# Gate modulation rows on TensorE, one inverse chain for both superchunks, and bonus products on ScalarE and GpSimd

## The chip, the cores and the metric

The kernel runs on one core of a Trainium2 chip (trn2). A core has a matrix engine (TensorE, PE in the profile), a vector engine (VectorE, DVE), a scalar engine (ScalarE, ACT), a general one (GpSimd, POOL) and a queue that issues transfers (SyncE, SP); each has its own instruction stream, and they meet at semaphores. Matrices come from HBM to SBUF (128 partitions) by DMA, and matmuls write to PSUM, of which there are eight banks of 128 x 512 floats. The metric is device time in microseconds, the median of several runs; smaller is better.

## What is computed

One layer of a network on 256 tokens of 1024 channels, in float32: a modulation from a conditioning vector c (twelve rows of 512 values, `silu(c) @ w_ada + b_ada`), a mixing block of which one half of the channels goes through a recurrence (RWKV-7) and the other through attention, a mixture of 32 experts with top 4, and a last block with memory. What the change touches is the following.

```python
# modulation: six vectors of 1024 values (twelve rows of 512)
ada = silu(c) @ w_ada + b_ada       # shift1, scale1, gate1, shift2, scale2, gate2
x = x + gate1 * mix(rms_norm(x) * (1 + scale1) + shift1)
h = rms_norm(x) * (1 + scale2) + shift2
x = x + gate2 * experts(h)

# recurrence, per head, over 256 steps
state = (state * w_t + (state @ -kk_t) x (kk_t * a_t) + v_t x k_t)
y_t = state @ r_t
bonus = sum(r * k * r_k, axis=-1) * v
y = (norm(y) + bonus) * g
```

The recurrence is computed in chunks: within one, the steps depend on each other through a lower triangular matrix, which has to be inverted.

## The kernel before

**Stages.** `phase1` does everything up to the routing, in about 300 us; then the experts run, whose weights (192 tiles of 2 MB) stream through SBUF, and then the last block. A tile scheduler orders the instructions of each engine from the program; a pool with `bufs=n` gives a tile n buffers, and a tile's next use waits until its last reader is done. All weight tiles go through `stream` (L138), which issues one 2 MB transfer on SyncE's queue into a ring of three buffers.

**Modulation.** `ada_rows` (L278) makes up to four of the twelve rows at once on TensorE. For each row it streams a 1024 x 512 piece of w_ada and issues eight matmuls, 128 x 32 weights against 128 x 512 (L285), one group of 32 PSUM partitions for each k mod 4; scw holds silu(c) in one column among zeros, so that row i lands in partition i of its group. A first matmul (L280) puts the bias in, and ScalarE copies the bank to SBUF. This serves rows 0 to 3 at the start (`ra` and its second call) and rows 6 to 9 (`r1`) after the projections. Rows 4, 5, 10 and 11, the two gates, are made otherwise, in `gate_rows` (L295): VectorE makes 4 and 10 with a product and seven fused multiply-adds of 128 x 512 into gacc (L307, L305), and GpSimd makes 5 and 11 with eight products (L307) and seven sums (L309). gacc is 8 KB in each partition. What is left over the partitions is summed and spread by a matmul with ones (`gate_bc`, L316), at the end of the attention block.

**Projections.** `dense_T` and `dense_N` multiply the input (split into two parts hh and hl) by a 1024 x 512 piece of w_in. For each of eight k the piece is split: ScalarE rounds it (wsh, L145) and VectorE, or for each fourth one GpSimd, makes the residue (wsl, L146); then three products go to TensorE (L396 to L399, L411 to L413). The order is the LoRA columns, k, r, v, then the attention's q, k and v. The LoRA weights wua and gup (L441 to L443) feed small matmuls lo (L453) and g (L461), whose results go through sigmoids and exponentials on ScalarE.

**Recurrence.** It has two superchunks s of 128 tokens. `sub` (L537) makes the triangular products of each; its 16 x 16 diagonal blocks are inverted by `invert(s, r)` (L556), r from 0 to 14: TensorE spreads row r (row, L565, with a selector sel that GpSimd makes, L564), and VectorE does a product (L570) and a sum (L572), each 128 x 8(15 - r). The two chains alternate. `sub2(s)` (L645) transposes v, a, b and k (tr, L658; b and k after a VectorE product dc, L653), makes the masked products (lk, L534 to L669), and more products lv, yv and zk; `solve(s)` (L694) does the rest of the inverse with f (L710) and u (L720), and the state follows. Attention heads (sc, pt, po) run between. The bonus product prod is four VectorE instructions (L639).

**After it.** `w_out` multiplies by the output weights, the gates are applied, `choose` and `rank` do the routing. SyncE's queue has by then issued nine tiles of expert weights; the tenth stands behind a load of the largest count of the routing into a register (L978, `values_load`), which decides a branch later on.

Of the kernel before, what the change touches and what calls it, by code (L numbers as in the profile page):

```python
# [10 lines left out]
F32 = mybir.dt.float32  # L11
# [3 lines left out]
AF = mybir.ActivationFunctionType  # L15
OP = mybir.AluOpType
# [3 lines left out]
T, D = 256, 1024  # L20
# [2 lines left out]
BIG = 3.0e38  # L23

SIG_MAX = 1.0 / (1.0 + math.exp(-1.702 * 7.0))


NP, B4, NZ, ME = 4, 5, 5, 12
# [91 lines left out]
class Kernel:  # L120
# [133 lines left out]
    def phase1(self):  # L254
# [23 lines left out]
        def ada_rows(cis):  # L278
# [11 lines left out]
            r = p1.tile([128, 512], F32, tag="ar", name="ar")  # L290
# [4 lines left out]
        sc = scw[:, :, 32]  # L295

        def gate_rows():

            for q, i in enumerate((4, 5, 10, 11)):
                w = self.stream(A["w_ada"][:, i * 512:(i + 1) * 512].rearrange("(k p) f -> p k f", p=128), 8, 512)  # L300
# [9 lines left out]
                r = slice(32 * q, 32 * q + 1)  # L310
                eng.tensor_tensor(o[r], o[r], self.gate2[r, 512:1024], op=OP.add)

        def gate_bc(q):
# [13 lines left out]

        xn = pxn.tile([128, 2, D], F32, tag="xn", name="xn")
        ss = p1.tile([128, 2], F32, tag="ss", name="ss")
        for q, i in enumerate((4, 5, 10, 11)):  # L330
# [207 lines left out]
        def sub(s):  # L538

            tt = slice(s * 128, s * 128 + 128)  # L540
            L16 = pb.tile([128, 8, 128], F32, tag="L16", name="L16")
            Lof = pb.tile([128, 8, 128], F32, tag="Lof", name="Lof", bufs=2)
            for p, ps in pairs(aT, bT, tt, "lab"):
                DVE.tensor_tensor(par(L16, p), ps, bc("m16", 4), op=OP.mult)
                DVE.tensor_tensor(par(Lof, p), ps, bc("moff", 4), op=OP.mult)
            Lc = pb.tile([128, 8, 16], F32, tag=f"Lc{s}", name="Lc")
# [3 lines left out]
            ACT.activation(Lc.rearrange("p h q -> p (h q)"), ps[:, 0:128], AF.Copy)  # L550

            Tc = pb.tile([128, 8, 16], F32, tag=f"Tc{s}", name="Tc")
            POOL.tensor_copy(Tc, e16[:, None, :].to_broadcast([128, 8, 16]))
            return Lof, Lc, Tc

        def invert(s, r):  # L556

            Lof, Lc, Tc = parts[s]
            if r % 4 == 0:
                rows[s] = self.psum("row", chain=True)  # L560
                for q in range(r, min(r + 4, 15)):
                    if s == 0:
                        sel[q] = pb.tile([128, 128], F32, tag="sel", name="sel", bufs=5)
                        POOL.tensor_scalar(sel[q], blk16, e16[:, q:q + 1], None, op0=OP.mult)  # L564
                    PE.matmul(rows[s][:, (q % 4) * 128:(q % 4) * 128 + 128], sel[q], Lc.rearrange("p h q -> p (h q)"),  # L565
                              start=True, stop=True, skip_group_check=True)
            n = 15 - r
            t = pb.tile([128, 8, 16], F32, tag=f"tq{s}", name="tq")
            o = (r % 4) * 128
            DVE.tensor_tensor(t[:, :, 0:n], rows[s][:, o:o + 128].rearrange("p (h q) -> p h q", h=8)[:, :, r + 1:16],  # L570
                              Tc[:, :, r:r + 1].to_broadcast([128, 8, n]), op=OP.mult)
            DVE.tensor_tensor(Tc[:, :, r + 1:16], Tc[:, :, r + 1:16], t[:, :, 0:n], op=OP.add)  # L572

        parts = [sub(s) for s in range(2)]
        parts2, rows, sel = {}, {}, {}
        for r in range(15):
            for s in range(2):
                invert(s, r)


        qn, kn2 = Y[:, 0], Y[:, 1]
# [54 lines left out]
        POOL.tensor_tensor(wr, wr, sc2[:, :, None].to_broadcast([128, 8, NE]), op=OP.mult)  # L636

        for m in range(4):
            DVE.scalar_tensor_tensor(prod[:, m], rT[:, m], self.v("rk", m), kT[:, m], op0=OP.mult, op1=OP.mult)  # L639

        pb1 = right("pb1", eC)
        big4 = lambda n: pb1.tile([128, 8, 128], F32, tag="b4", name=n, bufs=B4)
# [49 lines left out]
            return nat["b"], R, Lrb  # L692

        def solve(s):  # L694
            Lof, Lc, Tc = parts[s]
            nb, R, Lrb = parts2[s]
            D2 = big4("Dt")
            Dt = D2.rearrange("p h (b q) -> p h b q", q=16)
            for hf in range(2):
                hsl = slice(4 * hf, 4 * hf + 4)  # L700
                (POOL if hf else DVE).tensor_tensor(
                    Dt[:, hsl], Tc[:, hsl, None, :].to_broadcast([128, 4, 8, 16]),
                    blk16.rearrange("p (b q) -> p b q", q=16)[:, None].to_broadcast([128, 4, 8, 16]), op=OP.mult)
            Ft, Rp = big4("Ft"), big4("Rp")
            R2 = R.rearrange("p h a j -> p h (a j)")
# [181 lines left out]
                todo = []  # L887

        w_out((4, 5, 6, 7))
        for dst, q in ((gate, 0), (self.gate2, 2)):  # L890
            for h in range(2):
                ACT.activation(dst[:, h * 512:(h + 1) * 512], gate_bc(q + h), AF.Copy)
        eN.close()
        e2s.close()
        w_out((0, 1, 2, 3))
# [722 lines left out]
```

## Time and profile before

| what | value |
|---|---|
| median of 3 runs | 1542.88 us (1541.7 to 1546.55) |
| the profiled execution | 1553.07 us, of which the span is 1551.3 us |
| TensorE busy | 1425.1 us, 92% of the span |
| VectorE busy | 570.8 us, 37% |
| ScalarE busy | 396.5 us, 26% |
| GpSimd busy | 213.0 us, 14% |
| transfers | 505.17 MB, mean 326 GB/s |

The profile is of one execution, and it is 10.2 us longer than the median. Its page cuts the span into 40 slices of 38.8 us. The first seven and a half hold `phase1`, the next 23 the experts, the rest the last block. In a timeline row the first two numbers are the start and the length in us, the count after x is that of the instructions put together, and a bracket at the end tells how long the engine was idle ahead and what released it. TensorE records a float32 matmul as two instructions here, so x16 is eight matmuls. The granted clock (PEclk) is a share of full speed: 1.00 is 2.4 GHz and 0.50 is 1.2 GHz.

### The profile page before, as it was taken

The numbers are of one execution on the slowest core, as the hardware profiler recorded it, in microseconds if no ns is written. First come the engines' busy times: TensorE is split into PE (matmuls) and PEld (weight loads), VectorE is DVE, ScalarE is ACT, GpSimd is POOL, SyncE is SP. The second block draws the span as 40 slices with busy tenths as digits, with TensorE's granted clock in tenths as the row PEclk, the third lists the DMA queues.
The fourth block names the chain that finished last, engine by engine and source line by source line (L and its number), as shares of the span: only waits on it lengthen the run. The fifth ranks groups of instructions, "written<-read, shape, count | busy, mean of one in ns | idle before, by whom it ended". The sixth has DMA issues, their size and how long they took to land. (4 is left out here: it accounts for less than half of the span.)

```text
span 1551.3 us, 19123 instructions
## 1 busy us (share of the span) xinstructions
PE 1425.1 (92%) x7818; PEld 824.2 (53%) x7818; DVE 570.8 (37%) x1144; ACT 396.5 (26%) x767; POOL 213.0 (14%) x190
## 2 busy tenths in 40 slices
PE   5999999899999999888888879999998899899996
PEld 2976887533443344233233234443332597699995
DVE  3576766522222222122122122121211345565445
ACT  4862244200100000000000011110100466455553
POOL 1244751000000000000000000000000343252221
PEclk8999789899999999999999999999999999999998
DMA  9835726799999999999999999999999741535440
GB/s 332 271 109 177 261 78 259 326 429 427 428 427 429 426 429 426 427 429 427 428 429 426 427 421 428 428 427 428 428 426 426 269 164 55 217 111 210 169 164 28
DMA packets 74599, 505.17 MB, mean 326 GB/s; under 512 B 5661, under 2 KB 6685, under 8 KB 50025
## 3 DMA queue, kind: packets, MB, share of 16 engines
q1 hardware_dynamic: 74328, 503.74, 79.6%
q8 instruction: 63, 1.03, 0.3%
q14 instruction: 32, 0.25, 0.0%
q0 software_dynamic: 176, 0.14, 0.0%
HBM read 502.82 MB, written 1.05 MB: 325 GB/s over the span
## 5 line engine op out<-in xcount | busy, mean ns | idle before, releaser
L114 PE MATMUL pg<-w,xe 128*64 128x512 f32 x1024 | 270.5, 598 | 42.6 <-DMA w<-w_gate_up 42.1
L114 PE MATMUL pu<-w,xe 128*64 128x512 f32 x1024 | 268.2, 594 | 0.0
L114 PE MATMUL py<-w,at 128*64 128x512 f32 x1024 | 228.8, 599 | 23.8 <-ACT at L1167 20.6
L1155 ACT ACTIVATE sg<-pg 128x512 f32<-128x512 f32 (+1 forms) x33 | 19.3, 586 | 664.9 <-PE pg L114 663.2
L1156 DVE TENSOR_SCALAR u<-pu 128x512 f32<-128x512 f32 (+1 forms) x33 | 22.2, 676 | 450.7 <-PE pu L114 450.7
L114 PEld LDWEIGHTS pg<-w,xe 128*64 128x64 f32 x1024 | 71.6, 137 | 189.4 <-issue 116.4
L114 PEld LDWEIGHTS py<-w,at 128*64 128x64 f32 x1024 | 71.1, 137 | 158.7 <-issue 130.2
L114 PEld LDWEIGHTS pu<-w,xe 128*64 128x64 f32 x1024 | 75.4, 137 | 146.1 <-issue 145.9
L145 ACT ACTIVATE w3h<-w 128x512 fp32r<-128x512 f32 x184 | 115.4, 631 | 108.6 <-PE d L1309 57.8
L146 DVE TENSOR_TENSOR w3l<-w,w3h 128x512 fp32r<-128x512 f32 x132 | 97.1, 741 | 111.2 <-ACT w3h L145 106.2
L146 POOL TENSOR_TENSOR w3l<-w,w3h 128x512 fp32r<-128x512 f32 x52 | 67.5, 1303 | 421.5 <-ACT w3h L145 410.2
L1180 DVE TENSOR_TENSOR y<-py,gate 64x512 f32<-64x512 f32 x64 | 44.0, 688 | 207.8 <-PE py L114 207.0
L1309 PE MATMUL d<-xl,w3h 128*128 128x256 f32 x352 | 99.6, 284 | 0.4 <-DVE xl L1297 0.4
L1308 PE MATMUL d<-xh,w3h 128*128 128x256 f32 x352 | 99.0, 283 | 1.0 <-ACT xh L1295 1.0
L1310 PE MATMUL d<-xh,w3l 128*128 128x256 f32 x352 | 99.3, 283 | 0.0
L1244 POOL TENSOR_TENSOR wml<-w,wml 128x512 fp32r<-128x512 f32 x4 | 5.1, 1279 | 679.1 <-ACT wml L1243 679.1
L114 PEld LDWEIGHTS ga<-s,xm 128*128 128x128 f32 x512 | 63.2, 201 | 13.5 <-issue 11.9
L1308 PEld LDWEIGHTS d<-xh,w3h 128*128 128x128 f32 x352 | 67.3, 192 | 1.6 <-ACT xh L1295 1.3
L1309 PEld LDWEIGHTS d<-xl,w3h 128*128 128x128 f32 x352 | 67.5, 192 | 1.0 <-DVE xl L1297 0.6
L1310 PEld LDWEIGHTS d<-xh,w3l 128*128 128x128 f32 x352 | 67.4, 192 | 0.2 <-DVE w3l L146 0.2
L114 PE MATMUL ga<-s,xm 128*128 128x128 f32 x512 | 66.3, 289 | 1.2 <-DVE s L1106 1.2
L114 PE MATMUL cb<-y,swt 128*128 128x512 f32 x128 | 59.2, 605 | 0.8 <-DVE y L1180 0.8
(420 smaller groups left out, 2078.5 us busy)
## 6 DMA issues: line engine op xcount, KB each, us to landing
w<-w_gate_up SPq DMA_DIRECT2D x128, 2048.0 KB, 30.5
w<-w_down SPq DMA_DIRECT2D x71, 2048.0 KB, 27.4
w<-w_ada SPq DMA_DIRECT2D x12, 2048.0 KB, 9.2
w<-w_up SPq DMA_DIRECT2D x8, 2048.0 KB, 7.5
w<-w_in SPq DMA_DIRECT2D x6, 2048.0 KB, 12.8
w<-w_in_sb SPq DMA_DIRECT2D x5, 2048.0 KB, 16.6
w<-w_out SPq DMA_DIRECT2D x4, 2048.0 KB, 7.7
w<-w_mem_kv SPq DMA_DIRECT2D x1, 2048.0 KB
```

The source lines that it names most:

```text
L114: return self._keep(self.tc.nc.tensor.matmul(*a, **k))
L145: self.nc.scalar.activation(hi, src, AF.Copy)
L146: eng.tensor_tensor(lo, src, hi.bitcast(F32), op=OP.subtract)
L1155: ACT.activation(cut(s, c), cut(pg, c), AF.Sigmoid, scale=1.702)
L1156: DVE.tensor_scalar(cut(u, c), cut(pu, c), 8.0, -6.0, op0=OP.min, op1=OP.max)
L1180: DVE.tensor_tensor(st[e & ~1][2][r, hs], py[64 * h:64 * h + 64], self.gate2[64 * h:64 * h + 64, hs], op=OP.mult)
L1244: (POOL if k % 2 else DVE).tensor_tensor(wl, w[:, k], wh.bitcast(F32), op=OP.subtract)
L1308: PE.matmul(o, wh[:, ws], xh[:, k], start=k == 0 and i % 2 == 0, stop=False, skip_group_check=True)
L1309: PE.matmul(o, wh[:, ws], xl[:, k], start=False, stop=False, skip_group_check=True)
L1310: PE.matmul(o, wl[:, ws], xh[:, k], start=False, stop=k == 7, skip_group_check=True)
```

## The change

The four gate rows go through `ada_rows`, as rows 0 to 3 and 6 to 9 do, and stand in an SBUF tile of their own tag; `gate_bc` picks a row with the selector sel32 instead of summing with ones. gacc and four small transfers of b_ada on GpSimd's queue go away, and a memset of one row comes in. The two inverses become one chain over a tile of both superchunks, with all fifteen selectors made at once. prod becomes four scaled copies on ScalarE and one product on GpSimd.

```diff
-        gacc = p1.tile([128, 4, 512], F32, tag="gacc", name="gacc")
-        def gate_rows():
-            for q, i in enumerate((4, 5, 10, 11)):
-                w = self.stream(A["w_ada"][:, i * 512:(i + 1) * 512]...)
-                o, eng = gacc[:, q], POOL if q % 2 else DVE
-                for k in range(8):
-                    c = sc[:, k:k + 1]
-                    if eng is DVE and k:
-                        DVE.scalar_tensor_tensor(o, w[:, k], c, o, op0=OP.mult, op1=OP.add)
-                    else:
-                        eng.tensor_scalar(w[:, k] if k else o, w[:, k], c, None, op0=OP.mult)
-                        if k:
-                            eng.tensor_tensor(o, w[:, k], o, op=OP.add)
...
-            PE.matmul(ps, self.k("ones"), gacc[:, q], start=True, stop=True)
+            PE.matmul(ps, self.k("sel32")[:, i:i + 1].to_broadcast([128, 128]), rg, start=True, stop=True)
...
-            nc.gpsimd.dma_start(self.gate2[32 * q:32 * q + 1, 512:1024], A["b_ada"][i:i + 1])
+        POOL.memset(bada[0:1], 0.0)
...
+        Lc, Tc = (pb.tile([128, 2, 8, 16], F32, tag=n, name=n) for n in ("Lc", "Tc"))
+        sel = []
+        for q in range(15):
+            sel.append(pb.tile([128, 128], F32, tag="sel", name="sel", bufs=SB))
+            POOL.tensor_scalar(sel[q], blk16, e16[:, q:q + 1], None, op0=OP.mult)
-        def invert(s, r):
+        def invert(r):
-            if r % 4 == 0:
+            if r % 2 == 0:
+                rows[0] = self.psum("row", chain=True)
+                for q in range(r, min(r + 2, 15)):
+                    PE.matmul(rows[0][:, (q % 2) * 256:(q % 2) * 256 + 256], sel[q],
+                              Lc.rearrange("p s h q -> p (s h q)"), start=True, stop=True, ...)
...
+            DVE.tensor_tensor(t[:, :, 0:n], rows[0][:, o:o + 256]...[:, :, r + 1:16],
+                              T[:, :, r:r + 1].to_broadcast([128, 16, n]), op=OP.mult)
+            DVE.tensor_tensor(T[:, :, r + 1:16], T[:, :, r + 1:16], t[:, :, 0:n], op=OP.add)
...
-        gate_rows()
+        rg = ada_rows((4, 5, 10, 11), "ag")
...
-            DVE.scalar_tensor_tensor(prod[:, m], rT[:, m], self.v("rk", m), kT[:, m], op0=OP.mult, op1=OP.mult)
+            ACT.activation(prod[:, m], rT[:, m], AF.Copy, scale=self.v("rk", m))
+        POOL.tensor_tensor(prod, prod, kT, op=OP.mult)
```

What this does to the order of the instructions is not all in the diff. On TensorE, from the last steps of the inverse to the first solve, the order before is this (a piece of the first superchunk's products and of the solve):

```order
L285 MATMUL ada<-w,gate_74 32x512 x8
L658 MATMUL tr<-ca,vT 128x128 x4
L658 MATMUL tr<-ca,lent 128x128 x4
L658 MATMUL tr<-ca,dc 128x128 x4
L323 MATMUL adac<-ca,ar 128x4 x4
...
L710 MATMUL f<-Dt,Lof 128x128 x4
L710 MATMUL f<-lent,Dt 128x128 x3
L634 MATMUL cv<-wr,sh_72 128x32 x8
```

The same stretch after the change (the lines are shifted: L288 is ada, L640 tr, L654 lv, L615 cv, L692 f):

```order
L640 MATMUL tr<-ca,dc 128x128 x4
L288 MATMUL ada<-w,gate_74 32x512 x8
L640 MATMUL tr<-ca,dc 128x128
...
L654 MATMUL lv<-nv,Lak 128x64 x6
L288 MATMUL ada<-w,gate_74 32x512 x8
L654 MATMUL lv<-nv,Lak 128x64 x2
...
L615 MATMUL cv<-wr,sh_72 128x32 x8
L516 MATMUL lk<-G,lent 128x128 x8
L654 MATMUL lv<-nv,Lak 128x64 x8
```

Five groups of eight ada matmuls (the last of r1 and the four gate streams) now stand among the transposes and products of the two superchunks, and cv stands ahead of the second superchunk's lv instead of inside the first solve.

On ScalarE, at the end of the LoRA projection, the order before is this (pm is the shifted copy of the LoRA results, xwa the tanh, xg the sigmoid):

```order
L145 ACTIVATE wsh<-w 128x512 x4
L430 ACTIVATE pm_279<-pj,vec 128x256
L145 ACTIVATE wsh<-w 128x512
L430 ACTIVATE pm_281<-pj,vec 80x256
L145 ACTIVATE wsh<-w 128x512
L430 ACTIVATE pm_280<-pj,vec 80x256
L445 ACTIVATE xwa<-xwa 64x256
```

After the change it is:

```order
L412 ACTIVATE pm_275<-pj,vec 128x256
L412 ACTIVATE pm_277<-pj,vec 80x256
L412 ACTIVATE pm_276<-pj,vec 80x256
L427 ACTIVATE xwa<-xwa 64x256
L147 ACTIVATE wsh<-w 128x512 x5
L428 ACT_TABLE_LOAD
L428 ACTIVATE xg<-xg 80x512
L437 ACTIVATE lent<-lo,vec 128x256 x4
```

The copies and the tanh moved ahead of the splits of the next projection (k), and the first four LoRA sigmoids (lent from lo) now stand in k's stage; before they came after all eight of k's splits.

On GpSimd, at the turn from the recurrence's preparation to the inverse, the order before is this:

```order
L146 TENSOR_TENSOR wsl<-w,wsh 128x512
L513 TENSOR_TENSOR lent<-lent,e_917 128x512
L553 COPY Tc<-cb 128x128 x2
L564 TENSOR_SCALAR sel<-cb 128x128 x5
L146 TENSOR_TENSOR wsl<-w,wsh 128x512 x2
L564 TENSOR_SCALAR sel<-cb 128x128 x5
```

After the change it is:

```order
L148 TENSOR_TENSOR wsl<-w,wsh 128x512
L621 TENSOR_TENSOR rT<-rT,lent 128x1024
L495 TENSOR_TENSOR lent<-lent,e_913 128x512
L148 TENSOR_TENSOR wsl<-w,wsh 128x512
L536 COPY Tc<-cb 128x256
L540 TENSOR_SCALAR sel<-cb 128x128 x15
L148 TENSOR_TENSOR wsl<-w,wsh 128x512
```

The bonus product (rT) came in ahead of the second half of the decayed k (lent), and ten selectors moved ahead of the last residue product of w_in.

## Rows read from the trace of the kernel before

**Rows 1.** The page's slices of the span: what the transfer engines moved, in GB/s.

```profile
GB/s 332 271 109 177 261 78 259 326 429 427 428 427 429 426 429 426 427 429 427 428 429 426 427 421 428 428 427 428 428 426 426 269 164 55 217 111 210 169 164 28
```

**Rows 2.** Windows: length, busy of PE, PEld, DVE, ACT, POOL, granted clock, DMA, GB/s.

```profile
160.00:170.00 10.00, 10.00 (x124) 8.99 (x124) 9.66 (x21) 2.77 (x6) 3.60 (x3) 1.00 1.03 379
170.00:180.00 10.00, 8.44 (x70) 7.15 (x66) 9.89 (x16) 2.85 (x6) 10.00 (x6) 0.76 0.70 226
180.00:190.00 10.00, 10.00 (x66) 9.21 (x64) 6.57 (x10) 1.86 (x4) 10.00 (x7) 0.50 0.35 113
292.00:300.00 8.00, 8.00 (x50) 4.03 (x50) 4.61 (x15) 2.97 (x6) 0.00 (x0) 1.00 0.20 41
```

**Rows 3.** SyncE's queue at L978: durations in ns, then first and last start in us.

```profile
L978 SPq TENSOR_LOAD <-cmi x1: 479/479/479, 296.9 to 296.9; - x1
```

**Rows 4.** Timeline of TensorE: start, us, operation, output and inputs, shapes, wait before.

```profile
147.20 1.05 PE L285 MATMUL ada<-w,gate 128*32 128x512 f32 x2
...
156.81 1.92 PE L285 MATMUL ada<-w,gate 128*32 128x512 f32 x16
158.66 0.66 PE L658 MATMUL tr<-ca,vT 128*128 128x128 f32 x4
...
170.19 0.66 PE L658 MATMUL tr<-ca,vT 128*128 128x128 f32 x4
...
173.28 0.30 PE L658 MATMUL tr<-ca,dc 128*128 128x128 f32 x1 [1.56 <-DVE dc L653]
...
187.61 2.07 PE L710 MATMUL f<-Dt,Lof 128*128 128x128 f32 x8
...
190.75 3.46 PE L634 MATMUL cv<-wr,sh 128*128 128x32 f32 x16
...
201.16 1.73 PE L720 MATMUL u<-Rp,Ft 128*128 128x128 f32 x8
...
220.42 1.16 PE L710 MATMUL f<-Dt,Lof 128*128 128x128 f32 x8
...
225.78 1.16 PE L720 MATMUL u<-Rp,Ft 128*128 128x128 f32 x8
```

**Rows 5.** VectorE: gate accumulations grouped, busy us and mean ns; the bias row, timeline.

```profile
L305 DVE SCALAR_TENSOR_TENSOR gacc<-w,gate,gacc 128x512 f32<-128x512 f32 x14 | 13.0, 926 | 0.2
...
171.88 1.05 DVE L311 TENSOR_TENSOR gacc<-gacc,gate 1x512 f32<-1x512 f32 x1
```

**Rows 6.** Timeline of VectorE: scalings of the attention weights, two instructions each.

```profile
199.56 0.54 DVE L801 TENSOR_SCALAR s<-s,st 128x128 f32<-128x128 f32 x2
...
217.35 1.64 DVE L801 TENSOR_SCALAR s<-s,st 128x128 f32<-128x128 f32 x2
...
220.54 2.20 DVE L801 TENSOR_SCALAR s<-s,st 128x128 f32<-128x128 f32 x2
```

**Rows 7.** Timeline of GpSimd: ten gate sums in a row.

```profile
217.57 12.44 POOL L309 TENSOR_TENSOR gacc<-w,gacc 128x512 f32<-128x512 f32 x10
```

**Rows 8.** Timeline of VectorE: two of the bonus products.

```profile
102.93 2.92 DVE L639 SCALAR_TENSOR_TENSOR rT<-rT,vec,lent 128x256 f32<-128x256 f32 x2
```

**Rows 9.** Timeline of TensorE in the attention's k projection, behind those products.

```profile
107.61 0.80 PE L413 MATMUL pn<-wsl,hh 128*128 128x512 f32 x1 [2.39 <-DVE wsl L146]
108.20 0.63 PE L411 MATMUL pn<-wsh,hh 128*128 128x512 f32 x1
...
113.74 0.44 PE L412 MATMUL pn<-wsh,hl 128*128 128x512 f32 x1
```

**Rows 10.** Timeline of ScalarE: first splits of k, ends of k and r.

```profile
45.91 2.20 ACT L145 ACTIVATE wsh<-w 128x512 fp32r<-128x512 f32 x4 [2.92 <-DMA w<-w_in]
...
58.59 0.48 ACT L430 ACTIVATE pm<-pj,vec 128x256 f32<-128x256 f32 x1 [0.21 <-PE pj L399]
...
77.69 0.48 ACT L430 ACTIVATE pm<-pj,vec 128x256 f32<-128x256 f32 x1 [0.20 <-PE pj L399]
```

**Rows 11.** Timeline of VectorE: the first product of the inverse.

```profile
137.16 0.28 DVE L570 TENSOR_TENSOR tq<-row,Tc 128x120 f32<-128x120 f32 x1 [1.96 <-PE row L565]
```

More of the change, by code (lines that the diff above doesn't have):

```diff
@@ L25 @@
 SIG_MAX = 1.0 / (1.0 + math.exp(-1.702 * 7.0))
+SB = 15
 NP, B4, NZ, ME = 4, 5, 5, 12
@@ L276, in phase1, with ada_rows @@
         pxn = self.pool("pxn", es=eL)
-        def ada_rows(cis):
+        def ada_rows(cis, tag="ar"):
             ps = self.psum("ada")
@@ L289, in ada_rows, with gate_bc @@
                     self.expert_bias(pxn)
-            r = p1.tile([128, 512], F32, tag="ar", name="ar")
+            r = p1.tile([128, 512], F32, tag=tag, name="ar")
             ACT.activation(r, ps, AF.Copy)
             return r
-        gacc = p1.tile([128, 4, 512], F32, tag="gacc", name="gacc")
-        sc = scw[:, :, 32]
-        def gate_rows():
-            for q, i in enumerate((4, 5, 10, 11)):
-                w = self.stream(A["w_ada"][:, i * 512:(i + 1) * 512].rearrange("(k p) f -> p k f", p=128), 8, 512)
-                o, eng = gacc[:, q], POOL if q % 2 else DVE
-                for k in range(8):
-                    c = sc[:, k:k + 1]
-                    if eng is DVE and k:
-                        DVE.scalar_tensor_tensor(o, w[:, k], c, o, op0=OP.mult, op1=OP.add)
-                    else:
-                        eng.tensor_scalar(w[:, k] if k else o, w[:, k], c, None, op0=OP.mult)
-                        if k:
-                            eng.tensor_tensor(o, w[:, k], o, op=OP.add)
-                r = slice(32 * q, 32 * q + 1)
-                eng.tensor_tensor(o[r], o[r], self.gate2[r, 512:1024], op=OP.add)
-        def gate_bc(q):
+        def gate_bc(i):
             ps = self.psum("adab", chain=True)
-            PE.matmul(ps, self.k("ones"), gacc[:, q], start=True, stop=True)
+            PE.matmul(ps, self.k("sel32")[:, i:i + 1].to_broadcast([128, 128]), rg, start=True, stop=True)
             return ps
@@ L329, in phase1 @@
         ss = p1.tile([128, 2], F32, tag="ss", name="ss")
-        for q, i in enumerate((4, 5, 10, 11)):
-            nc.gpsimd.dma_start(self.gate2[32 * q:32 * q + 1, 512:1024], A["b_ada"][i:i + 1])
         ra = ada_rows((0, 2))
@@ L545, in sub @@
                 DVE.tensor_tensor(par(Lof, p), ps, bc("moff", 4), op=OP.mult)
-            Lc = pb.tile([128, 8, 16], F32, tag=f"Lc{s}", name="Lc")
             ps = self.psum("lc", chain=True)
@@ L549, in sub @@
                 PE.matmul(ps[:, h * 16:(h + 1) * 16], L16[:, h], e16, start=True, stop=True, skip_group_check=True)
[L550 to L554, printed above, removed]
-        def invert(s, r):
-            Lof, Lc, Tc = parts[s]
-            if r % 4 == 0:
[L560 to L566, printed above, removed]
-            n = 15 - r
[L568 to L572, printed above, removed]
@@ L574, in phase1 @@
-        parts = [sub(s) for s in range(2)]
-        parts2, rows, sel = {}, {}, {}
+            ACT.activation(Lc[:, s].rearrange("p h q -> p (h q)"), ps[:, 0:128], AF.Copy)
+            return Lof
+        Lc, Tc = (pb.tile([128, 2, 8, 16], F32, tag=n, name=n) for n in ("Lc", "Tc"))
+        POOL.tensor_copy(Tc.rearrange("p s h q -> p (s h) q"), e16[:, None, :].to_broadcast([128, 16, 16]))
+        sel = []
+        for q in range(15):
+            sel.append(pb.tile([128, 128], F32, tag="sel", name="sel", bufs=SB))
+            POOL.tensor_scalar(sel[q], blk16, e16[:, q:q + 1], None, op0=OP.mult)
@@ new lines, in invert @@
+        def invert(r):
[3 more added lines that the diff above has]
+                    PE.matmul(rows[0][:, (q % 2) * 256:(q % 2) * 256 + 256], sel[q],
+                              Lc.rearrange("p s h q -> p (s h q)"), start=True, stop=True, skip_group_check=True)
+            n = 15 - r
+            t = pb.tile([128, 16, 16], F32, tag="tq", name="tq")
+            o = (r % 2) * 256
+            T = Tc.rearrange("p s h q -> p (s h) q")
+            DVE.tensor_tensor(t[:, :, 0:n], rows[0][:, o:o + 256].rearrange("p (h q) -> p h q", h=16)[:, :, r + 1:16],
+                              T[:, :, r:r + 1].to_broadcast([128, 16, n]), op=OP.mult)
+            DVE.tensor_tensor(T[:, :, r + 1:16], T[:, :, r + 1:16], t[:, :, 0:n], op=OP.add)
@@ L576, in phase1 @@
+        parts, parts2, rows = [sub(s) for s in range(2)], {}, {}
         for r in range(15):
-            for s in range(2):
-                invert(s, r)
+            invert(r)
         qn, kn2 = Y[:, 0], Y[:, 1]
@@ L694, in solve @@
         def solve(s):
-            Lof, Lc, Tc = parts[s]
+            Lof, Ts = parts[s], Tc[:, s]
             nb, R, Lrb = parts2[s]
@@ L889, in phase1 @@
         w_out((4, 5, 6, 7))
-        for dst, q in ((gate, 0), (self.gate2, 2)):
+        for dst, i in ((gate, 4), (self.gate2, 10)):
             for h in range(2):
-                ACT.activation(dst[:, h * 512:(h + 1) * 512], gate_bc(q + h), AF.Copy)
+                ACT.activation(dst[:, h * 512:(h + 1) * 512], gate_bc(i + h), AF.Copy)
         eN.close()
```

2 lines of the change are left out of this document (1 added, 1 removed).

## The prediction

> **What bounds the kernel now.** I read the slices of the whole span first, then engine by engine the stretch that the change touches. From the eighth slice on the core draws 421 to 429 GB/s, slice after slice, until the experts' weights are through [rows 1]: that long stage is bound by the transfers of expert weights, and its length does not depend on any engine. What can change is when it starts. Between 292 and 300 us the transfer engines are busy 0.20 of the time [rows 2]: nine tiles of expert weights have been fetched ahead, and the SyncE queue holds the rest back behind one register load of the routing's result (L978), which runs at 296.9 [rows 3]. So whatever makes the path from the first projections to the routing shorter moves the start of the full-rate stage, and with it the end, by the same amount. The question is therefore what the edits do on the path up to 296.9 us.
>
> On that path I look at TensorE between 141 and 243 us. Its busy share is full, but the granted clock is 1.00 in 160 to 170, 0.76 in 170 to 180 and 0.50 in 180 to 190 [rows 2]: it ran at 2.4 GHz and then at 1.2 GHz. The fall follows a wait of 1.56 us at 173.28 for a VectorE product dc [rows 4], and VectorE was late because its gate accumulation occupied it until after 171.88 [rows 5]. Eight f matmul records take 2.07 us at 187.61 and 1.16 us for the same eight at 220.42 [rows 4]; so the low clock stretches the work by 2.07/1.16 = 1.78. With a window at 0.76, about half of 170 to 180 was at the low level, so it began at about 175.2.
>
> **Gate rows to TensorE (term D).** VectorE loses fourteen accumulations of 926 ns, 13.0 us [rows 5], beside two first products and two bias rows; GpSimd loses the same for its two rows. TensorE gains four streams of eight 32x512 matmuls; eight of them stand at 156.81 and the next work begins at 158.66, so a stream costs 1.85 us [rows 4]. The order puts one more stream, the last of r1, from ahead of the transposes to behind them; so 5 x 1.85 = 9.3 us stand between the first transposes and the solve. The cv matmuls (3.46 us at the low clock, 3.46/1.78 = 1.9 at the high one) move ahead of the solve too.
>
> At the high clock the sum is: the first superchunk, 170.19 - 158.66 = 11.5 us; the second took 187.61 - 170.19 = 17.4, of which 1.6 is the wait and 12.4 (from 175.2) ran at the low clock and would take 7.0, so 10.4; the five streams 9.3; cv 1.9. From 158.7 that puts the first f at 191.8, where it was 187.61. From f to the first u the other superchunk's solve needs 225.78 - 220.42 = 5.4 us at the high clock; before, at the low one and with cv inside, it was 201.16 - 187.61 = 13.6 [rows 4]. u then starts at 197.2 instead of 201.16: **-4.0 us**. The w_ada streams land later than before, since a ring tile is refilled only when TensorE has read it; I find them there just before they are wanted, so I price that wait at nothing, with up to +3 us if each comes half a microsecond or so late. TensorE takes its work in order, so behind a stream that is late stand the transposes and the lk products that VectorE wants.
>
> The switch of tile shape could cost too. A single such matmul between rows, at 147.20, took 1.05 us, where eight together cost 0.23 each [rows 4]. The Trainium skill (TensorEngine Tiling (Array Packing), section Key Properties) says that changing the tiling mode drains TensorE, which speaks against putting these groups among the transposes; at 0.8 us each that would make five groups 4.1 us dearer and the sum about 1540. The eight at 156.81, with other shapes on both sides, took 8 x 0.23, so the row does not bear that price out for groups of eight. I take 0.
>
> **Products off VectorE (term B).** The four products of r, k and the bonus weight leave VectorE; two of them took 2.92 us at 102.93 [rows 8], and right behind them stands the residue wsl for which TensorE waits 2.39 us at 107.61. Behind that wait thirteen 512-column matmuls start between 108.20 and 113.74, 0.43 us each [rows 9], where eight of 512 columns took 0.23 each at the high clock: 13 x 0.2 = 2.6, with the first some 2.8 us lost. The wait goes with the products; the slow clock behind it probably does, but another short wait could keep it. **-3.9 us**, between -2.4 and -5.2. ScalarE gets four scaled copies, at 0.48 us by its like [rows 10], and has idle time there. GpSimd gets one 128x1024 product, about twice the 1.24 us of its 128x512 sums [rows 7], and the fifteen selectors in one run ahead of one residue product of w_in v; behind them waits at most one TensorE step: 0 to +2, I take 0 because the ring holds five splits. The Trainium skill (SBUF — State Buffer, section SBUF: two separate sides) says that a GpSimd instruction that reads SBUF and a VectorE one with two SBUF inputs exclude each other for a whole instruction; by that rule the moved product would take about 2.5 us back from VectorE and leave B at -1.4, the sum at about 1539.
>
> **One inverse chain (term C).** Sixty small VectorE products become thirty of double size, all dependent. The first, of 120 elements, takes 0.28 [rows 11]; thirty between that and its double, falling in size, average about 0.33, some 10 us in all. TensorE's rows, 15 of 256 columns instead of 30 of 128, feed the same columns in half the instructions, so they cost no more. In before TensorE goes through rows and gate matmuls in turn, without a wait, from ahead of 147.20 until 158.66 [rows 4], 11.5 us and more; a chain of 10 us fits beside that. The chain's last steps wait for rows that come behind gate matmuls in twos and threes, and the rows before them come earlier; a lone gate matmul cost 1.05 instead of 0.23, so I allow 0.8 us either way and take **0**.
>
> **Less strife late (term E).** GpSimd's ten sums from 217.57 to 230 [rows 7] go. While they ran, two scalings that take 0.54 us took 1.64 and 2.20 [rows 6], 2.8 us on VectorE in all; TensorE had other work behind some of it. **-1.0 us**, 0 to -2.
>
> **What comes along (term A).** Without gacc the LoRA weights need no longer wait for memory, so their matmuls, sigmoids and table loads stand in the dense stage of k instead of that of r. In before the stage of k runs from 45.91 to 58.59, that of r with all of this inside to 77.69, 19.1 us [rows 10]: moving the work from one to the other is free by itself. But ScalarE then does its three pm copies and the tanh before the first splits of k, and TensorE's first LoRA matmuls stand ahead of k's own. Before, four splits of 2.20 us in all stood ahead; that cover is gone: **+2.1 us**, 0 to +5, since the weights of k also land behind those of the LoRA.
>
> At nothing: the broadcast matmuls at the end (same count), the four small GpSimd transfers at the start, the memset in their place, and the second w_out tile, which is issued earlier but is used only when y is done.
>
> **Sum.** +2.1 - 3.9 + 0 - 4.0 - 1.0 = -6.8 us on a profiled execution of 1553.1, that is 1546.3. The timed runs have a median of 1542.9, 10.2 less; I carry the difference over: **1536 us**.
>
> **The rivals.**
> (1) *TensorE stays at the low clock.* The same thin work (64-row tiles) is still there from 170 on, and TensorE could pause for a stream. If the clock falls at 175.2 as before, 22.0 us of work are left to u at 197.2; at 1.78 that puts u at 214.4 if the clock doesn't rise before it, or at 208.6 if it rises 26 us later, where before's u began: D = +7.4 to +13.2, the sum +4.6 to +10.4. That gives 1547 to 1553, 1550 for one number: slower. It decides when TensorE stops for more than a microsecond between 165 and 180. For it: it did in before. Against it: the wait for VectorE goes.
> (2) *The timed runs never had the low clock there.* The profiled execution is 10.2 us longer than the median, and the low clock from 175.2 to 201.16 and beyond is worth about 26 x (1 - 1/1.78) = 11.4 us. Then before's u is at about 190, TensorE is what ends last in the stretch, and 9.3 us of gate matmuls come onto it while only the wait of 1.6 goes: D = +7; with B at -2.4, since the slow clock at 108 may be missing too, the sum is about +5.5, that is 1548. Against it: the three runs lie within 5 us, as they would if the same happened in each, and the difference could as well lie in the long transfer-bound stage; no row here tells.
> (3) *The small terms cancel.* A at +5, B at -2.4 and E at 0 leave, with D at -4.0, -1.4: 1541, no change. This is also the case in which the change does little of what it says.
>
> **How the numbers follow.** A measurement of this kernel can tell about 0.3%, 4.6 us, from no change. Forecast 0.45, own range 1531 to 1541 (faster 0.36, within 0.3% 0.09); rival 1 0.25 (within 0.06, slower 0.19); rival 2 0.17 (0.06, 0.11); rival 3 0.13 (faster 0.05, within 0.07, slower 0.01). That gives faster 0.41, within 0.28, slower 0.31. The range reaches from the low end of the forecast to the top of rival 1: 1530 to 1553.
>
> **What would show it.** Right: no wait for dc and a granted clock near 1.00 from 160 to 200; u about 4 us earlier at its own place in the trace; no wait of 2.4 us for wsl near 107; the scalings at 0.54 us throughout the second solve; the start of the stage of r about 2 us later; L978 at about 290. Wrong: a clock of 0.50 among the second superchunk's products (rival 1); a profiled execution that gains while the timed runs do not (rival 2); TensorE idle before an ada matmul with the w_ada transfer as releaser.

## The result: 20 us slower, and the profile after

The changed kernel has a median of 1563.55 us (4 runs, 1560.19 to 1566.57), the kernel before 1543.72 (4 runs, 1541.7 to 1546.55): a ratio of 1.0126, interval 1.011 to 1.0143. The prediction was 1536 us, faster; the measured time lies beyond the top of its range.

The page's slices answer to [rows 1]: the experts still run at 427 to 428 GB/s.

```profile
GB/s 317 230 160 109 304 185 162 219 420 428 427 428 427 427 427 427 428 428 427 428 428 427 426 423 428 427 428 427 428 427 428 303 162 54 215 108 200 177 162 27
```

Execution times of one kernel mostly go with the clock that TensorE was granted in them, so its mean over the span stands beside some times here. The profile of the kernel before that the prediction read had a mean clock of 0.970 and took 1553.07 us. The unchanged kernel was therefore profiled again: 1543.91 us, mean clock 0.982. From here on "before" is that second profile.

SyncE's register load (it was L978, it is L960 now; [rows 3] shows it at 296.9 in the first profile), before and after; the columns are those of [rows 3].

```profile
L978 SPq TENSOR_LOAD <-cmi x1: 483/483/483, 287.5 to 287.5; - x1
L960 SPq TENSOR_LOAD <-cmi x1: 478/478/478, 311.1 to 311.1; - x1
```

The load is 23.6 us later, the span 1564.8 - 1542.1 = 22.7 us longer. What lies behind the load hasn't changed by more than 0.9 us, as the prediction said; all of the loss is ahead of it. VectorE is busy 552.5 us now and GpSimd 166.0, so the work did leave them: [rows 5, 7] have no counterpart. TensorE is busy 1432.7. The table takes it apart by TensorE's starts in the timelines (us).

| stretch on TensorE | first profile | before | after | after - before |
|---|---|---|---|---|
| start to first attention product pn | 90.19 | 91.42 | 93.97 | +2.6 |
| pn to the first transpose tr | 68.47 | 70.90 | 73.03 | +2.1 |
| tr to tr of the second superchunk | 11.53 | 11.53 | 17.92 | +6.4 |
| that to the first f | 17.42 | 11.95 | 21.14 | +9.2 |
| first f to the first u | 13.55 | 7.16 | 7.41 | +0.3 |
| u to the routing's last cast, just ahead of the load | 95.59 | 94.42 | 97.43 | +3.0 |

From tr to u it is 30.6 us before and 46.5 after: 15.8 of the 23.5. The profiled execution of the changed kernel is itself the slowest of its four runs, 3.0 us above their median, so some of this is its own. The windows answer to [rows 2]; first before, then after, same columns.

```profile
170.00:180.00 10.00, 8.88 (x109) 7.72 (x109) 9.82 (x17) 3.77 (x8) 9.78 (x5) 1.00 0.72 256
180.00:190.00 10.00, 10.00 (x109) 9.34 (x109) 9.93 (x14) 2.78 (x6) 10.00 (x8) 1.00 0.36 112
190.00:200.00 10.00, 10.00 (x73) 8.04 (x70) 9.02 (x27) 5.79 (x21) 10.00 (x7) 1.00 0.97 373
```

```profile
180.00:190.00 10.00, 9.52 (x112) 5.78 (x113) 0.90 (x4) 3.45 (x7) 0.00 (x0) 1.00 0.82 283
190.00:200.00 10.00, 10.00 (x81) 7.44 (x79) 4.52 (x10) 1.19 (x2) 0.62 (x1) 0.98 0.89 296
200.00:210.00 10.00, 10.00 (x64) 9.21 (x65) 0.37 (x1) 2.29 (x5) 0.00 (x0) 0.51 0.84 336
```

The 0.50 in 180 to 200 of the first profile isn't there before: the clock is 1.00, although VectorE is busy throughout and TensorE waits for dc. After, VectorE has almost nothing to do (0.37 us of ten), and the clock is 0.51. TensorE's timeline shows both prices in their place (after; columns as in [rows 4]).

```profile
167.93 0.60 PE L640 MATMUL tr<-ca,dc 128*128 128x128 f32 x4
168.46 1.93 PE L288 MATMUL ada<-w,gate 128*32 128x512 f32 x16
...
185.40 1.92 PE L288 MATMUL ada<-w,gate 128*32 128x512 f32 x16
...
188.93 0.30 PE L640 MATMUL tr<-ca,dc 128*128 128x128 f32 x1 [0.48 <-DVE dc L635]
...
195.99 1.97 PE L615 MATMUL cv<-wr,sh 128*128 128x32 f32 x16
197.89 1.71 PE L516 MATMUL lk<-G,lent 64*128 64x128 f32 x16
199.53 3.65 PE L654 MATMUL lv<-nv,Lak 128*128 128x64 f32 x16
203.11 1.98 PE L660 MATMUL yv<-Lrk,nv 128*64 128x128 f32 x16
205.01 1.12 PE L670 MATMUL zk<-nv,nk 64*64 64x64 f32 x16
206.06 2.07 PE L692 MATMUL f<-Dt,Lof 128*128 128x128 f32 x8
...
213.47 1.16 PE L702 MATMUL u<-Rp,Ft 128*128 128x128 f32 x8
```

And before:

```profile
160.47 1.92 PE L285 MATMUL ada<-w,gate 128*32 128x512 f32 x16
162.32 0.66 PE L658 MATMUL tr<-ca,vT 128*128 128x128 f32 x4
...
176.50 0.30 PE L658 MATMUL tr<-ca,dc 128*128 128x128 f32 x1 [1.12 <-DVE dc L653]
...
182.21 2.00 PE L672 MATMUL lv<-nv,Lak 128*128 128x64 f32 x16
184.14 1.09 PE L678 MATMUL yv<-Lrk,nv 128*64 128x128 f32 x16
185.19 0.68 PE L688 MATMUL zk<-nv,nk 64*64 64x64 f32 x16
185.80 1.16 PE L710 MATMUL f<-Dt,Lof 128*128 128x128 f32 x8
...
192.96 1.06 PE L720 MATMUL u<-Rp,Ft 128*128 128x128 f32 x8
```

The five streams are there, two of them shown: 5 x 1.85 = 9.3 us. The same products lv, yv, zk and f take 8.82 us after and 4.93 before: at 1.2 GHz 3.9 us more, and 0.85 more for the f behind them. Against that stands the wait for dc, 1.12 before and 0.48 after. That makes 13.4 of the 15.8; the rest is spread over the stretch and not itemised.

The low clock isn't a fixed part of the price. The changed kernel with five selector buffers (e7_sb5 below) keeps the high clock there, with the same work in the stretch:

```profile
200.00:210.00 10.00, 10.00 (x96) 8.67 (x95) 4.77 (x14) 6.20 (x19) 0.00 (x0) 1.00 0.90 333
```

It takes 39.6 us from tr to u, 8.9 more than before. Five streams less the wait for dc, which it doesn't have, come to 9.25 - 1.12 = 8.1.

### The profile page after: what moved, and what is told of

Its sections match the earlier page's. It is cut to its first block, busy times and chain, and to the rows that moved or that the text cites. A ratio compares the mean times of both kernels' runs of the same rounds, so it can differ in the third digit from the quotient of the medians.

```text
span 1564.8 us, 19101 instructions
## 1 busy us (share of the span) xinstructions
PE 1432.7 (92%) x7854; PEld 822.3 (53%) x7854; DVE 552.5 (35%) x1092; ACT 397.0 (25%) x772; POOL 166.0 (11%) x155
## 3 DMA queue, kind: packets, MB, share of 16 engines
HBM read 502.81 MB, written 1.05 MB: 322 GB/s over the span
## 5 line engine op out<-in xcount | busy, mean ns | idle before, releaser
L116 PEld LDWEIGHTS ga<-s,xm 128*128 128x128 f32 x512 | 63.1, 200 | 13.4 <-issue 11.8
```

The costliest lines, as they stand in the source:

```text
L116: return self._keep(self.tc.nc.tensor.matmul(*a, **k))
```

## The experiments

All stand against the kernel before on the same chip. The clocks are those of the single executions.

| run | ratio | interval | median us (runs) | mean clock |
|---|---|---|---|---|
| e0_before | 1.0009 | 0.9989 to 1.0029 | 1544.24 (10) | 0.974 to 0.983 |
| e3_gates | 1.0093 | 1.0076 to 1.0109 | 1557.61 (4) | 0.976 to 0.979 |
| e4_lora_kept | 1.0055 | 1.0037 to 1.0073 | 1552.9 (4) | 0.976 to 0.978 |
| e5_double | 1.0144 | 1.0127 to 1.0161 | 1566.58 (4) | 0.979 to 0.981 |
| e1_prod | 1.0006 | 0.9987 to 1.0025 | 1545.27 (10) | 0.975 to 0.982 |
| e6_no_prod | 1.0099 | 1.0068 to 1.013 | 1559.07 (5) | 0.971 to 0.984 |
| e2_inverse | 1.0045 | 1.002 to 1.007 | 1547.64 (10) | 0.971 to 0.981 |
| e7_sb5 | 1.0125 | 1.0104 to 1.0146 | 1562.62 (4) | 0.975 to 0.979 |
| e10_change_kept | 1.0134 | 1.0092 to 1.0177 | 1564.96 (4) | 0.971 to 0.979 |
| e8_early | 0.9995 | 0.9973 to 1.0018 | 1543.86 (10) | 0.976 to 0.984 |
| e9_early_prod | 1.0032 | 1.0004 to 1.006 | 1547.6 (10) | 0.976 to 0.985 |
| e11_row5_first | 1.0066 | 1.0045 to 1.0087 | 1556.27 (4) | 0.971 to 0.978 |

**The kernel before, unchanged.**

> The kernel before, unchanged, profiled and timed again. Theory 1 (the losses of the change lie in waits that its own trace shows: 3.8 us by the end of the stage of r, 4.8 us in the attention's projections, 4 us between the transposes and u, 1.9 us behind): the second profile shows the same low clock from about 175 to 201 and a span near 1551, and the timed runs are as before. Theory 2 (the low clock between 175 and 201 was not there in the timed runs, so the gate matmuls cost more than the two traces show): the second profile or the timed runs show a mean granted clock of 0.977 or more and a span about 10 us shorter.

Nine of its ten runs took 1540.9 to 1546.4 us; the tenth took 1555.81 at a mean clock of 0.974. Of the 59 runs of it that served as reference for the experiments two were above 1548 (1552.95 and 1553.22), and none had a mean clock below 0.977. So the first profile, at 0.970, shows a rare execution, and as far as the mean clocks tell its low clock from 175 on was no part of the median that the prediction carried its sum over to.

**The gates alone.** The kernel before with the four gate rows on TensorE and nothing else; gacc goes, so the LoRA work moves too.

```diff
-        gate_rows()
+        rg = ada_rows((4, 5, 10, 11), "ag")
```

> The kernel before with the gate rows alone moved to TensorE; gacc goes, so the LoRA work moves into the stage of k as in the changed kernel. Theory 1: +3.8 us by the end of the stage of r, and about +6 between the transposes and the end of the routing, +8 to +10 in all, half of the whole change. Theory 2: +12 to +15 in the timed runs and less in the profile. Rival (my terms A and D): -2 us.

Measured 1.0093, three quarters of the whole loss. The clock is 1.00 from 160 to 210 in its profile, so what it shows is the plain price of the work: from tr to u 37.6 us instead of 30.6. Four streams stand there, 4 x 1.85 = 7.4, the dc wait is 0.47 instead of 1.12, and 7.4 - 0.65 = 6.8 of the 7.0 are found.

```profile
185.14 0.30 PE L638 MATMUL tr<-ca,dc 128*128 128x128 f32 x1 [0.47 <-DVE dc L633]
...
186.01 1.92 PE L286 MATMUL ada<-w,gate 128*32 128x512 f32 x16
...
194.75 2.00 PE L652 MATMUL lv<-nv,Lak 128*128 128x64 f32 x16
```

**The gates, with the LoRA work kept in the stage of r.** The same with a tile of 6 KB in each partition that nothing reads, so that memory is as short as with gacc.

```diff
+        spare = p1.tile([128, 1536], F32, tag="spare", name="spare")
+        DVE.memset(spare[0:1, 0:8], 0.0)
```

> The gates on TensorE as in e3_gates, with a spare tile of 6 KB a partition that takes the memory that gacc left, so that the LoRA work stays in the stage of r. Theory 1 (the gates cost only the TensorE time of their matmuls; the stage of r ended 0.2 us later in e3_gates than in e0_before): the same as e3_gates within 2 us, 1.0093 against before. Rival (my term A, +2.1, or the 3.8 us that the changed kernel's first trace shows): 2 to 4 us faster than e3_gates, 1.0065 to 1.008.

1.0055 against 1.0093: the two kernels are 4.7 us apart by the medians, 5.9 by the ratios. From tr to u this kernel takes 37.6 us too, so the price of the gate matmuls is separate from this. From the adac near 36 to pn it takes 52.4 us, the gates alone 56.5: 4.1 us for the LoRA move itself. At u the two profiles are 5.1 us apart: the gates alone start that stretch 1.7 us earlier, and lose 2.7 more between pn and tr, where TensorE waits 3.30 us for mqs instead of 1.91. The run with each matmul twice has the LoRA move too and waits 1.89 there, so those 2.7 us aren't shown to be the move's. What the move costs is seen in the windows of 35 to 40 us, before, after (there with 50 to 55) and of this run (last number GB/s), and in TensorE's and ScalarE's timelines after.

```profile
35.00:40.00 5.00, 4.22 (x34) 2.51 (x27) 1.44 (x6) 2.51 (x7) 1.11 (x3) 1.00 1.03 386
```

```profile
35.00:40.00 5.00, 2.38 (x18) 1.52 (x11) 0.80 (x4) 1.64 (x5) 0.00 (x0) 0.92 1.06 236
...
50.00:55.00 5.00, 3.77 (x22) 3.41 (x23) 4.31 (x7) 4.79 (x9) 1.42 (x1) 0.78 1.05 387
```

```profile
35.00:40.00 5.00, 4.21 (x36) 3.01 (x29) 2.06 (x6) 3.11 (x9) 1.00 (x1) 1.00 1.03 383
```

```profile
38.95 1.78 ACT L147 ACTIVATE wsh<-w 128x288 fp32r<-128x288 f32 x5 [2.52 <-DMA w<-w_in]
```

```profile
39.45 0.58 PE L378 MATMUL pj<-hh,wsh 128*128 128x256 f32 x1 [1.90 <-ACT wsh L147]
...
51.23 1.14 PE L435 MATMUL lo<-xwa,wua 64*128 64x256 f32 x8 [1.66 <-ACT xwa L427]
```

The transfer engines are busy and move 236 GB/s instead of 386 while the small LoRA weights are under way beside w_in, so the first piece of w_in is late and TensorE stands for 1.90 us. It then stands for 1.66 ahead of lo, where ScalarE does the copies and the tanh first, and the clock falls to 0.78. (In 40 to 45 it falls in both, to 0.66 before and 0.74 after.) With the spare tile the same weights are fetched later, behind work.

**Each gate matmul twice.** The kernel with the gates alone, and behind every matmul of the four gate rows one more with zero weights into the same bank, so that the sums stay what they are.

```diff
+                    if cis[0] == 4:
+                        PE.matmul(ps[32 * j:32 * j + 32, :], scw[:, k, 0:32], w[:, k, :], start=False,
+                                  stop=n == len(cis) - 1 and k >= 4, skip_group_check=True)
```

> The gates on TensorE as in e3_gates, with every one of their 32 matmuls issued a second time with weights that are all zero, so that the result stays. Theory 1 (TensorE's own time is the price, 1.85 us for each group of eight): +7.4 us on e3_gates, 1.014 against before. Rival (the price is the wait for the streams or for the ring's tiles): within 2 us of e3_gates.

It took 8.4 us (spans of the profiles) to 9.0 (medians) more than the gates alone, by the ratios 0.51% or 7.9, close to the 7.4 of four more streams. So TensorE's time in this stretch goes to the end almost one to one, and the low clock isn't needed to explain it: the mean clock of these runs is 0.979 to 0.981, above that of the gates alone.

**The bonus product alone, and the change without it.** The first is the kernel before with only this edit, the second the changed kernel with this edit undone.

```diff
-            DVE.scalar_tensor_tensor(prod[:, m], rT[:, m], self.v("rk", m), kT[:, m], op0=OP.mult, op1=OP.mult)
+            ACT.activation(prod[:, m], rT[:, m], AF.Copy, scale=self.v("rk", m))
+        POOL.tensor_tensor(prod, prod, kT, op=OP.mult)
```

> The kernel before with the bonus products alone moved (four scaled copies on ScalarE, one 128x1024 product on GpSimd). Theory 1: the product on GpSimd holds up a VectorE product for its whole length, as 2.80 and 2.83 us beside each other in the changed kernel show, and TensorE waits for what VectorE makes late: +1 to +4 us. Rival (my prediction's term B, VectorE is relieved): -2 to -5 us, and no wait of 2.4 us for wsl.

> The changed kernel with the bonus products back on VectorE (gates and one chain as changed). Theory 1 (the 128x1024 product on GpSimd blocks VectorE for 2.8 us and TensorE waits for that): 2 to 4 us faster than the changed kernel, 1.010 to 1.0115 against before. Rival (as e1_prod says, moving the products is neutral): 1.0126 within 1.5 us. My term B would make it slower, 1.014 or more.

Alone it is worth nothing (1.0006). Within the change it seems to cost some 4 us, 1.0126 against 1.0099, but the intervals overlap. The profiles point the same way: from pn to tr it is 2.6 us longer with the edit alone, 4.1 within the change and 7.0 in the pair e8_early and e9_early_prod below. The wait of 2.40 for wsl is gone in both kernels that have the edit, as predicted. In its place stand two others, the same in both (2.57 and 4.54 with the edit alone). Here are a product of the same shape before, with GpSimd idle, then GpSimd, VectorE and TensorE in the changed kernel:

```profile
109.32 0.68 DVE L511 TENSOR_TENSOR lent<-lent,e 128x512 f32<-128x512 f32 x1
```

```profile
118.32 2.80 POOL L621 TENSOR_TENSOR rT<-rT,lent 128x1024 f32<-128x1024 f32 x1
118.83 2.83 DVE L494 TENSOR_TENSOR lent<-lent 128x512 f32<-128x512 f32 x1
```

```profile
121.72 1.23 PE L516 MATMUL lab<-lent 64*128 64x128 f32 x8 [2.57 <-DVE lent L494]
127.50 2.01 PE L588 MATMUL mt<-ca,mqs 128*128 128x128 f32 x8 [4.55 <-DVE mqs L580]
```

VectorE's product at 118.83 (the second half of the decayed b) takes 2.83 us and ends half a microsecond after GpSimd's big product has ended; against 0.68 that gave back 2.15 us at once. The rule of the Trainium skill on this (SBUF — State Buffer, section SBUF: two separate sides), by which the two exclude each other for a whole instruction, is borne out by these two rows. TensorE waited 2.40 + 1.95 here before and waits 2.57 + 4.55 now, since VectorE's work ahead of mt comes later. The clock is 0.55 in 120 to 130, where it was 0.66; it is as low, 0.56 and 0.54, in the runs with the gates and the inverse alone, so that isn't the edit's.

**The inverse alone, and the change with five selector tiles.** In the first there are five selector buffers, since fifteen don't fit beside gacc; the second shows what that is worth.

```diff
-            for s in range(2):
-                invert(s, r)
+            invert(r)
```

```diff
-SB = 15
+SB = 5
```

> The kernel before with the one inverse chain alone, with five selector buffers as before, since fifteen don't fit beside gacc. Theory 1 and my term C: within 1.5 us of before, since the stretch from the end of the projections to the transposes was 17.6 us before and 17.4 in the changed kernel. Rival (the chain of thirty dependent VectorE products paces TensorE): +3 to +6 us.

> The changed kernel with five selector buffers instead of fifteen: GpSimd makes five ahead and the others when TensorE has used one. Theory 1 (fifteen selectors in one run, 11 us on GpSimd from 125.7, delay a residue product and VectorE's small products): 1 to 3 us faster than the changed kernel. Rival (the selectors are ready either way, and with five TensorE's rows break into more and smaller groups): 0 to 2 us slower than it.

The number of selectors is neutral (1.0125 against 1.0126). The one chain was priced at 0 and measured 1.0045 alone; part of this is clock: three of its ten runs took 1554.6 to 1559.9 at 0.971 to 0.973, the others 1544.8 to 1548.7. The order differs too: its last r1 stream stands behind the first transposes, at 162.55, and the stretch from pn to u is 104.6 us against 101.5. What the rest comes from isn't shown. With the gates on TensorE the chain makes no difference that could be told (1.0099 against 1.0093).

**The whole change with the LoRA work kept.** This one has five selector buffers, and a spare tile of 5 KB in each partition.

```diff
+        spare = p1.tile([128, 1280], F32, tag="spare", name="spare")
```

> The whole change, with five selector buffers (e7_sb5 showed that their number is neutral) and a spare tile of 5 KB a partition, so that the LoRA work stays in the stage of r. Theory (the parts add): the 3 to 6 us that the LoRA move cost between e3_gates and e4_lora_kept go, 1.0088 to 1.0105 against before. Rival (the LoRA move costs only in that company): as e7_sb5, 1.0125.

A miss: 1.0134, where the price of the LoRA move should have come off. In the profile it did come off ahead of pn (88.6 instead of 94.0), but that execution, the fastest of the four (1558.36 at 0.979), is only 1.8 us below the fastest of the changed kernel. The other three, at 0.971 and 0.972, took 1564.8 to 1566.7. So runs of one kernel differ by 6 to 8 us with the clock, and prices below that can't be added up across kernels. Even its profiled fastest run has a fall, with no wait of TensorE ahead of it:

```profile
180.00:190.00 10.00, 10.00 (x96) 7.56 (x93) 1.92 (x8) 3.43 (x7) 1.48 (x2) 0.90 0.72 241
190.00:200.00 10.00, 10.00 (x64) 9.66 (x64) 5.75 (x12) 1.58 (x5) 0.35 (x1) 0.50 0.99 389
```

**Three tries at something better, from the kernel before.** The first writes the first r1 stream ahead of the wait for mt; the second adds the bonus edit; the third has the first's order, with VectorE's gate rows 4 and 10 and GpSimd's row 11 written behind both superchunks' products.

```diff
+        def first():
+            early.append(ada_rows(range(6, 10), todo=(6,)))
...
-        gate_rows()
+        gate_row(5, gate_stream(5))
+        gw = [gate_stream(i) for i in (4, 10)]
...
+        for i, w in zip((4, 10), gw):
+            gate_row(i, w)
...
```

> The kernel before with one edit of its own: the first of r1's four w_ada streams, and its bias and eight matmuls, are written ahead of the first transposes mt of the attention's queries, for which TensorE waits 1.95 us in e0_before and behind which it runs at the low clock. Theory 1 (what counts in fast runs is TensorE's time and its waits): the eight matmuls fill that wait, the clock holds, and 1.9 us go from the stretch behind: -3 to -5 us, 0.997 to 0.998. Rival (the wait for mqs moves to the next place, or the w_in stream that now lands behind the w_ada stream is late): 0 to +3 us.

> As e8_early, with the bonus products moved as in the change. Theory 1 (the moved product takes the wait for wsl near 107 away and makes mt wait longer, which the matmuls now fill): 1 to 3 us faster than e8_early. Rival (the product on GpSimd keeps VectorE from the work that mt waits for): 0 to 3 us slower than e8_early.

> The kernel before with two changes of order and no change of work: the first stream of r1 (bias and eight gate matmuls) is written ahead of the wait for mt, as in the run with that alone, and VectorE's sums for the gate rows 4 and 10, with GpSimd's for row 11, are written behind the products of both superchunks; only row 5 (GpSimd) stays where it was. In the run with the early stream alone the stretch from the first attention product to the first transpose was 67.0 us long against 70.9, but that from the first transpose to the first u was 35.5 us against 30.6, so nothing was left at the end. Theory: that second stretch is then bound by VectorE, whose gate sums of 0.93 us stand among the products on which TensorE waits (dc above all); with them moved back it returns to 30.6 to 32, the routing's load comes 3 to 5 us earlier than in before, and the time is 1539 to 1541 us, a ratio of 0.997 to 0.998. Rival 1: the second stretch is bound by TensorE and by the w_ada transfers; then it stays at 35 and the ratio is 1.000. Rival 2: the low clock among the products of the second superchunk decides; then the granted clock of 170 to 200 is below 0.8 in the profile and the ratio is 1.002 to 1.005.

The first gains 3.9 us from pn to tr (67.0 against 70.9) and gives back 4.9 from tr to u (35.5 against 30.6), where its clock is low for some 7 us: no difference. With the bonus edit on it the ratio is 1.0032, some 0.4% higher again, with intervals that overlap a little. In the third, tr of the second superchunk starts at 168.46, 5.4 us ahead of before; then the theory falls, since the scheduler left row 4's sums ahead of dc on VectorE, and TensorE waits longer than ever, with the low clock behind it:

```profile
167.64 5.60 DVE L311 SCALAR_TENSOR_TENSOR gacc<-w,gate,gacc 128x512 f32<-128x512 f32 x6
173.16 3.06 DVE L666 TENSOR_TENSOR dc<-lent,ge 128x128 f32<-128x128 f32 x4
```

```profile
173.59 0.45 PE L671 MATMUL tr<-ca,dc 128*128 128x128 f32 x1 [3.60 <-DVE dc L666]
```

```profile
180.00:190.00 10.00, 10.00 (x55) 9.71 (x55) 7.02 (x10) 0.00 (x0) 6.60 (x5) 0.50 0.47 178
190.00:200.00 10.00, 10.00 (x59) 8.12 (x58) 4.39 (x9) 3.64 (x9) 10.00 (x7) 0.50 0.38 126
```

None of the three beats the kernel before.

**What stays open.** Why the clock falls among the 64-row products in one execution and not in another. It fell behind waits of 1.56 us (first profile), 3.60 (e11_row5_first) and 0.91 (e8_early, for some 7 us), but not behind 1.12, 1.27 and 1.07 (before, e1_prod, e2_inverse), and it fell in the changed kernel, in e9_early_prod and in e10_change_kept with no wait above 0.48 between tr and there. A wait for VectorE is therefore neither needed for it nor enough, and the cause isn't settled. It wasn't tried to hold the clock up.

## Why the prediction was wrong, point by point

**The bound** was right: the load of the routing's result sets the end, 23.6 us there and 22.7 in the span.

**Gates (D), forecast -4.0.** This step failed. The 9.3 us of streams were sized rightly (1.85 each, five of them), and so was the end of the dc wait. What failed is the credit against it: the prediction took the low clock of one execution, 175 to 201, for a property of the kernel and wrote it off as a gain. The sum for the new stretch held: 38.5 us from tr to u in the prediction, 39.6 measured at the clock of 1.00 (e7_sb5). What it was held against didn't: 42.5 us in the first profile, 30.6 in the second, with nearly all of the difference low clock. Rival 2 had the comparison that holds (D = +7): it is +8.9 in e7_sb5, and +7.0 in the gates alone, where only four streams stand in the stretch. Rival 2 was given 0.17, though the text itself noted that the profiled execution was 10.2 us longer than the median and that this low clock is worth 11.4. That was the row to go by. On top, the profiled execution of the changed kernel has a low clock of its own from 199.5 on, rival 1's mechanism a little later than rival 1 put it: 0.51 in 200 to 210, some 4.7 us. Its condition, a stop of TensorE, wasn't met.

**LoRA (A), +2.1, 0 to +5.** Right in kind and on the low side: +3.5 us from the adac at 36.49 to pn (57.48 against 53.95), and 4.1 in the pair of runs that differ in it alone, whose times are 4.7 to 5.9 apart. The prediction named the transfers that land later; what was missing is that they also slow w_in's own, and the 1.66 us ahead of lo.

**Products (B), -3.9.** The gain didn't come: 0 alone, and some +4 within the change, though not clear of noise. The wait for wsl went as forecast; the step that failed is GpSimd's part ("0 to +2, I take 0"): it cost the neighbour on VectorE 2.15 us, and TensorE two later waits, 7.1 us in place of 4.35. The -1.4 that the prediction worked out from the Trainium skill's rule was nearer than its own term.

**Inverse (C), 0.** Held where the gates are on TensorE; alone it cost about 0.45%, beyond the 0.8 us that were allowed.

**Less strife late (E), -1.0.** On VectorE it came, as the scalings of [rows 6] show, before and then after:

```profile
203.21 2.57 DVE L801 TENSOR_SCALAR s<-s,st 128x128 f32<-128x128 f32 x2
...
213.74 2.18 DVE L801 TENSOR_SCALAR s<-s,st 128x128 f32<-128x128 f32 x2
```

```profile
217.73 0.54 DVE L783 TENSOR_SCALAR s<-s,st 128x128 f32<-128x128 f32 x2
...
224.05 0.54 DVE L783 TENSOR_SCALAR s<-s,st 128x128 f32<-128x128 f32 x2
```

At the end it isn't seen: from u to the routing it is 3.0 us longer, and TensorE is busy 39.8 of the 40 us from 200 to 240.

The shares of the loss, read along one chain of kernels by their ratios: gates 0.55%, LoRA move 0.38, inverse 0.06, bonus product 0.27. They make 1.26% by construction, and the last two lie within the intervals. The run with the LoRA work kept in the whole change warns that these don't simply add.

## What to carry to other kernels

Hold the profiled execution against the timed runs first: if it is longer by as much as one odd feature in it is worth, the feature probably belongs to that execution, and no gain may be taken from its removal. Work moved from an engine that is waited for 1 us onto the one that waits is a loss of the whole work less that 1 us, and freed memory moves other work too. A product given to GpSimd can be paid by VectorE's instruction beside it, as the one at 118.83 was.

## What the runs showed of the hardware

Matmuls of 32 columns go four at a time: a group costs by rounds of four, not by the piece. In the inverse-alone run a record of x2 is one matmul and x24 are twelve:

```profile
148.14 2.78 PE L287 MATMUL ada<-w,gate 128*32 128x512 f32 x24
...
151.48 1.05 PE L287 MATMUL ada<-w,gate 128*32 128x512 f32 x2
...
155.12 1.06 PE L287 MATMUL ada<-w,gate 128*32 128x512 f32 x6
156.74 1.90 PE L287 MATMUL ada<-w,gate 128*32 128x512 f32 x10
```

One and three take 1.05, five take 1.90, twelve 2.78; to the start of the next work that is 0.98, 1.83 and 2.71, so 0.90 to 0.98 for each round of four begun. The prediction read [rows 4] as "0.23 each, and 0.8 more for a lone one"; the lone one is simply a round with three places empty. The Trainium skill says of this (TensorEngine Tiling (Array Packing), section Key Properties) that tiles work independently of each other, which agrees. It also says that changing the tiling mode drains TensorE; these rows need no price for that.

With the mean clock go 6 to 8 us among runs of the same kernel here (1558.36 at 0.979, 1564.79 to 1566.68 at 0.971 and 0.972 in e10_change_kept), a third or more of what the whole change cost.

While 64- and 80-partition transfers ran beside a stream of 2 MB tiles, the busy transfer engines moved 236 GB/s instead of 386 (35 to 40 us, after and before). With the LoRA work kept it is 383 there, and the fall comes later, with the transfers: 182 in 53 to 54, at a share of 1.01.
